# The first RMSNorm of a decoder trunk, from scheduler-ordered code to a written order

## The chip, the cores and the metric

One NeuronCore of a Trainium2 chip runs the kernel. The metric is the device time of one execution in microseconds (us), as the median of several runs. TensorE (PE in the profile, PEld for its weight loads) multiplies, VectorE (DVE) and ScalarE (ACT) do the elementwise work, GpSimd (POOL) takes some of it, and DMAs are issued from the queues of SyncE (SP) and ScalarE. Every time below counts from the first instruction of the profiled execution.

## The reference

Two layers of a decoder trunk over 512 tokens of 1024 channels, and a last norm. Each layer is

```python
for l in range(DEPTH):
    h = rmsnorm(x, norm_mix[l])
    proj = h @ w_in[l]
    pa, pb, pc, pd = split_cols(proj, [NSA_COLS, DIL_COLS, RWKV_COLS, CONV_COLS])
    ...
    x = x + jnp.concatenate([y_a, y_b, y_c, y_d], axis=-1) @ w_out[l]
    h = rmsnorm(x, norm_ffn[l])
    x = x + conv_ffn(h, ffn_up[l], ffn_dw[l], ffn_dw_b[l], ffn_down[l])
return rmsnorm(x, norm_final)

def rmsnorm(x, g):
    xf = x.astype(jnp.float32)
    y = xf * lax.rsqrt(jnp.mean(xf * xf, axis=-1, keepdims=True) + RMS_EPS)
    return (y * g).astype(x.dtype)
```

The four mixers (sparse attention, dilated attention, RWKV-7, a convolution) read `proj`. The change concerns the first `rmsnorm` of layer 0 and what feeds it.

## The kernel before

Channels lie on partitions: x is eight tiles of 128 channels by 512 tokens, in float32. Products run on float16 pairs: a value is a high part plus a low part, and one product of 128 channels is three matmuls (`mm3`, L221 to L223: weight high x hx high, weight high x hx low, weight low x hx high). A weight tile of 128 x 1024 float32 comes by DMA into a ring of two staging buffers (`st`); `_split` makes the high part on ScalarE (L200) and the low part on VectorE (L201), into a ring of five (`hl`).

The norm works in two halves of 256 tokens. For each half, ScalarE squares the eight x tiles (L363), VectorE or GpSimd adds the squares into two accumulators (L370), TensorE sums over channels by products with ones (L383), VectorE makes the inverse root in ten small steps on 128 x 2 values (L256 to L267), and two transposes on TensorE (L387) spread it over all channels. Then per tile k: VectorE scales x into `nt` (L401, a ring of three), ScalarE casts it to the high part of hx (L402), VectorE subtracts for the low part (L403).

The projection begins with `gemm_head`: four output tiles (wa, k0, r0, v0), each in a PSUM bank of its own (two of tag g, two of tag r), over the first half of the tokens, then over the second. The next tile, over all 512 tokens, takes the first bank again, once ScalarE (L411) and VectorE (L412) have read it.

A scheduler with a timeline of its own orders all instructions: it moves them past each other by their priority and by the times that it reckons with, so the order on an engine is not that of the code. The opening is written as

```python
self.norm_begin(ip, 4, 2)
for cols in self.HALVES:
    for k in range(NK):
        a1 = k % 3 == 1
        self.norm_add(k, cols, nc.gpsimd if a1 else nc.vector, int(a1))
    self.norm_apply(self.d["gm"], hx, cols)
```

with the loads of x and the first weight splits at high priority ahead of it, all from the queue of SyncE. The tables lora, cw2 and pos go out first on the queue of ScalarE.

## Time and profile before

| what | value |
|---|---|
| times of three runs | 1353.32, 1356.33, 1356.33 us (median 1356.33) |
| profiled execution: span on the page | 1353.0 us; its own time is not listed apart, the lowest run is 0.3 above |
| TensorE busy | 1301.1 us, 96% of the span |
| VectorE / ScalarE / GpSimd busy | 67% / 45% / 9% |
| first matmul of the projection | 19.01 us |
| first matmul behind the head | 42.30 us |

Busy time of TensorE is its modelled occupation, not useful work at peak. An engine's idle time costs something only where the chain that ends last passes through it. The mean granted clock of TensorE over the span is 0.988 of full speed.

### The profile page before, as it was taken

What the parts mean: (1) busy time and instruction counts of PE and PEld (TensorE: products, weight loads), DVE (VectorE), ACT (ScalarE), POOL (GpSimd) and SP (SyncE); (2) the same over time, 40 slices, a digit from 0 to 9 for tenths busy, and PEclk for the clock granted to TensorE, in tenths of its full rate; (3) what the DMA queues carried; (4) which work ended last, traced back from release to release, by engine and by line L of the source; (5) the groups of instructions that cost most, each with busy time, mean ns of one, the idle gap of its engine ahead of it and who ended that gap; (6) DMA issues with size and microseconds to landing.
All of it is one profiled execution on the core that took longest, in us unless ns stands there. A gap on an engine that the chain in (4) does not pass through costs nothing.

```text
span 1353.0 us, 22896 instructions
## 1 busy us (share of the span) xinstructions
PE 1301.1 (96%) x9198; PEld 737.9 (55%) x9198; DVE 910.4 (67%) x1770; ACT 609.3 (45%) x1115; POOL 119.5 (9%) x180
## 2 busy tenths in 40 slices
PE   5999999999999999999999998999999999999996
PEld 4545567656644444444674455775584444444445
DVE  6779985777777777632277899757678677774323
ACT  5544567644544444422245345766345444443220
POOL 2000022213000000001100001223110000000110
PEclk9999989999999999999999999999999999999998
DMA  6521400022233233333333223001214333333321
GB/s 221 162 79 59 125 26 10 1 71 94 93 94 109 93 109 94 102 120 118 109 129 124 66 79 102 10 3 32 78 49 128 105 103 100 106 93 102 98 86 63
DMA packets 41866, 119.97 MB, mean 89 GB/s; under 512 B 4896, under 2 KB 11680, under 8 KB 41760
## 3 DMA queue, kind: packets, MB, share of 16 engines
q1 hardware_dynamic: 35136, 110.50, 26.2%
q10 hardware_dynamic: 6624, 8.01, 1.8%
q8 instruction: 72, 1.18, 0.4%
q14 instruction: 34, 0.28, 0.1%
HBM read 114.30 MB, written 4.19 MB: 88 GB/s over the span
## 4 chain that ended last, share of the span: by engine, by line
PE 77%; DVE 15%; ACT 3%; DMA 2%; issue 2%; SPq 0%; ACTq 0%; DVEq 0%
PE g L222 20%; PE g L223 20%; PE g L221 20%; DVE cacc L733 4%; DVE hl L201 3%; PE v L900 3%; PE t L889 2%; PE s L869 2%; PE r L556 1%; DMA st<-in_wi_dram 1%; ACT hl L200 1%; PE r L222 1%; PE r L223 1%; DVE e L872 1%; PE r L221 1%
## 5 line engine op out<-in xcount | busy, mean ns | idle before, releaser
L221 PE MATMUL g<-hx,hl 128*128 128x512 f16 (+1 forms) x1024 | 373.7, 368 | 4.2 <-ACT hx L402 3.7
L222 PE MATMUL g<-hx,hl 128*128 128x512 f16 (+1 forms) x1024 | 374.5, 368 | 1.0 <-DVE hx L403 0.9
L201 DVE SCALAR_TENSOR_TENSOR hl<-st,hl 128x1024 f16<-128x1024 f32 (+2 forms) x200 | 239.9, 1199 | 201.0 <-ACT hl L200 200.7
L223 PE MATMUL g<-hx,hl 128*128 128x512 f16 (+1 forms) x1024 | 374.9, 368 | 0.0
L200 ACT ACTIVATE hl<-st 128x1024 f16<-128x1024 f32 (+2 forms) x200 | 206.0, 1031 | 272.7 <-PE g L223 227.7
L221 PEld LDWEIGHTS <-hl 128*128 128x128 f16 x1724 | 170.6, 99 | 162.9 <-issue 7.5
L223 PEld LDWEIGHTS <-hl 128*128 128x128 f16 x1724 | 169.8, 98 | 157.8 <-issue 2.4
L222 PEld LDWEIGHTS <-hl 128*128 128x128 f16 x1724 | 170.2, 99 | 155.2 <-issue 2.9
L222 PE MATMUL g<-act,hl 128*128 128x512 f16 (+1 forms) x396 | 140.7, 355 | 0.0
L223 PE MATMUL g<-act,hl 128*128 128x512 f16 (+1 forms) x396 | 140.7, 355 | 0.0
L221 PE MATMUL g<-act,hl 128*128 128x512 f16 (+1 forms) x396 | 140.7, 355 | 0.0
L733 DVE SCALAR_TENSOR_TENSOR cacc<-gl,d_cdw,cacc 128x511 f32<-128x511 f32 (+14 forms) x120 | 89.8, 748 | 1.4
L370 POOL TENSOR_TENSOR acc<-acc,sq 128x256 f32<-128x256 f32 (+1 forms) x38 | 44.0, 1157 | 465.9 <-ACT sq L363 409.8
L887 POOL TENSOR_SCALAR e<-e,den 128x512 f32<-128x512 f32 (+3 forms) x96 | 55.9, 596 | 316.6 <-DVE den L879 208.0
L1006 DVE SCALAR_TENSOR_TENSOR x<-g,x 128x512 f32<-128x512 f32 (+1 forms) x62 | 34.9, 568 | 67.2 <-PE g L223 67.2
L1089 ACT CAST act<-u 128x512 f16<-128x512 f32 x44 | 27.2, 618 | 114.0 <-DVE u L1087 114.0
L872 DVE CUSTOM_DVE_ANT_0 e<-s,con 128x512 f32<-128x512 f32 (+3 forms) x96 | 46.7, 487 | 33.7 <-PE s L869 25.0
L1085 ACT ACTIVATE fth<-u 128x512 f32<-128x512 f32 x44 | 27.6, 628 | 82.9 <-DVE u L1082 82.9
L1082 DVE SCALAR_TENSOR_TENSOR u<-g,d_fdw,u 128x510 f32<-128x510 f32 x84 | 62.8, 748 | 2.7
L1080 ACT ACTIVATE u<-g,par,d_fdw 128x512 f32<-128x512 f32 x84 | 64.0, 762 | 0.0
L1081 DVE SCALAR_TENSOR_TENSOR u<-g,d_fdw,u 128x511 f32<-128x511 f32 x84 | 62.5, 744 | 0.0
L876 ACT ACTIVATE e<-e,mx 128x512 f32<-128x512 f32 (+3 forms) x96 | 53.2, 556 | 16.2 <-DVE mx L874 16.1
(265 smaller groups left out, 1634.3 us busy)
## 6 DMA issues: line engine op xcount, KB each, us to landing
st<-in_up_dram SPq DMA_DIRECT2D x88, 512.0 KB, 3.5
st<-in_wi_dram SPq DMA_DIRECT2D x40, 512.0 KB, 3.4
st<-in_dn_dram SPq DMA_DIRECT2D x32, 512.0 KB, 3.5
st<-in_wo_dram SPq DMA_DIRECT2D x16, 512.0 KB, 3.5
st<-in_dn_dram SPq DMA_DIRECT2D x16, 384.0 KB, 3.1
w<-in_cw_dram ACTq DMA_DIRECT2D x16, 256.0 KB, 4.1
st<-in_wv_dram SPq DMA_DIRECT2D x8, 396.0 KB, 3.1
x<-in_x_dram SPq DMA_DIRECT2D x16, 128.0 KB, 3.5
```

The source lines that it names most:

```text
L200: nc.scalar.activation(hl[:, 0, :cols], st[:, :cols], AF.Copy, scale=SW)
L201: nc.vector.scalar_tensor_tensor(hl[:, 1, :cols], st[:, :cols], SW, hl[:, 0, :cols], op0=ALU.mult, op1=ALU.subtract)
L221: nc.tensor.matmul(ps, hl[:, 0, w], hx[:, 0, cols], start=start, stop=False)
L222: nc.tensor.matmul(ps, hl[:, 0, w], hx[:, 1, cols], start=False, stop=False)
L223: nc.tensor.matmul(ps, hl[:, 1, w], hx[:, 0, cols], start=False, stop=stop)
L733: nc.vector.scalar_tensor_tensor(acc[:, s:512], gl[:, 0:512 - s], wj, acc[:, s:512], op0=ALU.mult, op1=ALU.add)
L872: nc.vector.tensor_tensor_reduce(es[i], ps[:, o:o + w], mask[:, 384 - 128 * t:512], op0=ALU.add, op1=ALU.max, scale=1.0, scalar=-3e38, acc ...
L876: nc.scalar.activation(es[i], es[i], AF.Exp, scale=SC, bias=mx[:, i:i + 1], accum_out=den[:, i:i + 1])
L887: nc.gpsimd.tensor_scalar(es[i], es[i], den[:, i:i + 1], 1.0, op0=ALU.mult, op1=ALU.mult)
L1080: nc.scalar.activation(u, ps, AF.Identity, scale=w[:, 88 + ch:89 + ch], bias=self.p("fb", ch))
L1081: stt(u[:, 1:512], ps[:, 0:511], w[:, 44 + ch:45 + ch], u[:, 1:512], op0=ALU.mult, op1=ALU.add)
L1082: stt(u[:, 2:512], ps[:, 0:510], w[:, ch:ch + 1], u[:, 2:512], op0=ALU.mult, op1=ALU.add)
```

## The change

The opening of layer 0 moves into a function `open_x` inside a region in which the scheduler keeps the written order on each engine. In it, the first half of x is loaded from two queues in turn; the identity part of the constants, the parameters and two weight tiles follow, then the second half of x. Six of the eight squares of the first half are added by VectorE, alternating between the two accumulators, and the last two go as tiles of their own through the column sums (the ring of squares grows from four to six). The ten steps of the root stand in a row. The scaling, casts and low parts of the first half are interleaved with the two weight splits and with the squares of the second half; two of the low parts and all six adds of the second half are GpSimd's. The other constants and lora, cw2 and pos are loaded behind that. The second half then goes through the unchanged `norm_apply`. `layer_params` is cut into three functions that do the same for the later layers. Comments were dropped throughout.

```diff
+    def split_hi(self, st, cols):
+        nc = self.nc
         hl = self.whl.tile([128, 2, 1024], F16, tag="hl", name=self.n("hl"))
         nc.scalar.activation(hl[:, 0, :cols], st[:, :cols], AF.Copy, scale=SW)
-        nc.vector.scalar_tensor_tensor(hl[:, 1, :cols], st[:, :cols], SW, hl[:, 0, :cols],
-                                       op0=ALU.mult, op1=ALU.subtract)
-        return hl
+        return hl, lambda: nc.vector.scalar_tensor_tensor(hl[:, 1, :cols], st[:, :cols], SW, hl[:, 0, :cols],
+                                                          op0=ALU.mult, op1=ALU.subtract)
...
-        if l == 0:
-            self.nc.sync.dma_start(self.con[:, 128:], self.a["con"][:, 128:])
...
-            with tc.high_priority():
-                for i, cols in enumerate(self.HALVES):
-                    for k in range(NK):
-                        nc.sync.dma_start(self.x[k][:, cols], a["x"][:, k, cols])
-                    if i == 0:
-                        nc.sync.dma_start(self.con[:, :128], a["con"][:, :128])
-                        self.load_par(0)
-                    for _ in range(W_AHEAD):
-                        self.ready.append(self._split(*self.todo.pop(0)))
-            self.layer_params(0)
-            self.norm_begin(ip, 4, 2)
-            for cols in self.HALVES:
-                for k in range(NK):
-                    a1 = k % 3 == 1
-                    self.norm_add(k, cols, nc.gpsimd if a1 else nc.vector, int(a1))
-                self.norm_apply(self.d["gm"], hx, cols)
+            with tc.manual_schedule():
+                self.open_x(ip, hx)
...
+    def open_x(self, ip, hx):
+
+        nc, a = self.nc, self.a
+        h0, h1 = self.HALVES
+        load = lambda eng, k, cols: eng.dma_start(self.x[k][:, cols], a["x"][:, k, cols])
+        for k in range(NK):
+            load((nc.sync, nc.scalar)[k % 2], k, h0)
+        nc.sync.dma_start(self.con[:, :128], a["con"][:, :128])
+        self.load_par(0)
+        st = [self.w_load(*self.todo.pop(0)) for _ in range(2)]
+        for k in range(NK):
+            load(nc.sync, k, h1)
+        self.layer_consts()
+        self.norm_begin(ip, 6, 2)
+        for k in range(NK):
+            self.norm_add(k, h0, nc.vector if k < NK - 2 else None, k % 2)
+        hl0, lo0 = self.split_hi(st[0], 1024)
+        rb = self.norm_rb(h0)
+        nts = []
+        for k in range(NK + 1):
+            if k < NK:
+                nts.append(self.norm_mul(k, self.d["gm"], rb, h0))
+                nc.scalar.copy(hx[k][:, 0, h0], nts[k])
+                for i in {4: (0,), 5: (1, 2), 6: (3, 4), 7: (5, 6, 7)}.get(k, ()):
+                    self.norm_add(i, h1, nc.gpsimd, i % 2)
+            if k:
+                (nc.vector, nc.gpsimd)[k < 5 and k % 2 == 0].tensor_tensor(
+                    hx[k - 1][:, 1, h0], nts[k - 1], hx[k - 1][:, 0, h0], op=ALU.subtract)
+            if k == 1:
+                lo0()
+                self.ready.append(hl0)
+            if k == 4:
+                self.ready.append(self._split(None, 1024, st[1]))
+        for _ in range(2):
+            self.ready.append(self._split(*self.todo.pop(0)))
+        nc.sync.dma_start(self.con[:, 128:], a["con"][:, 128:])
+        self.layer_loads(0)
+        self.spread_done = None
+        self.norm_apply(self.d["gm"], hx, h1)
```

TensorE around the column sums of the second half (s is their bank, acc the accumulators, hl a split weight tile, g and r the banks of the head's tiles), before:

```order
L378 LDWEIGHTS zero
L378 MATMUL s_262<-zero 128x2
L383 MATMUL s_262<-ones,acc_165 128x1 x2
L383 MATMUL s_262<-ones,acc_166 128x1 x2
L221 LDWEIGHTS hl_119
L221 MATMUL g_344<-hx_79,hl_119 128x256
L221 LDWEIGHTS hl_132
L221 MATMUL g_345<-hx_79,hl_132 128x256
```

and now, further back, between the second and the third tile of the head:

```order
L226 LDWEIGHTS hl_262
L226 MATMUL r_352<-hx_79,hl_262 128x256
L395 MATMUL s_277<-ones,acc_155 128x1 x2
L225 LDWEIGHTS hl_267
L225 MATMUL r_353<-hx_79,hl_267 128x256
L226 LDWEIGHTS hl_267
L226 MATMUL r_353<-hx_79,hl_267 128x256
L395 MATMUL s_277<-ones,acc_156 128x1 x2
L227 LDWEIGHTS hl_262
L227 MATMUL r_352<-hx_79,hl_262 128x256
L225 LDWEIGHTS hl_262
L225 MATMUL r_352<-hx_80,hl_262 128x256
```

The sums stood ahead of all products; now they stand among the first products of the third and the fourth tile (r). From the last row of the sums to the transposes that spread the second root there are 41 products over 256 columns, which now stand between the two.

VectorE at the scaling of the second half (nt the scaled tile, hx the pair, t the spread root), before:

```order
L267 SCALAR_TENSOR_TENSOR y_271<-a_272,y_271 128x2
L403 TENSOR_TENSOR hx_86<-nt_238,hx_86 128x256
L401 SCALAR_TENSOR_TENSOR nt_285<-x_98,d_gm_141,t_263 128x256
L401 SCALAR_TENSOR_TENSOR nt_289<-x_99,d_gm_141,t_263 128x256
L401 SCALAR_TENSOR_TENSOR nt_293<-x_100,d_gm_141,t_263 128x256
L403 TENSOR_TENSOR hx_79<-nt_285,hx_79 128x256
L403 TENSOR_TENSOR hx_80<-nt_289,hx_80 128x256
L401 SCALAR_TENSOR_TENSOR nt_297<-x_101,d_gm_141,t_263 128x256
L403 TENSOR_TENSOR hx_81<-nt_293,hx_81 128x256
L401 SCALAR_TENSOR_TENSOR nt_301<-x_102,d_gm_141,t_263 128x256
L401 SCALAR_TENSOR_TENSOR nt_305<-x_103,d_gm_141,t_263 128x256
```

and now:

```order
L271 SCALAR_TENSOR_TENSOR y_286<-a_287,y_286 128x2
L206 SCALAR_TENSOR_TENSOR hl_342<-st_340,hl_342 128x1024
L410 SCALAR_TENSOR_TENSOR nt_300<-x_98,d_gm_131,t_278 128x256
L419 TENSOR_TENSOR hx_79<-nt_300,hx_79 128x256
L410 SCALAR_TENSOR_TENSOR nt_304<-x_99,d_gm_131,t_278 128x256
L419 TENSOR_TENSOR hx_80<-nt_304,hx_80 128x256
L410 SCALAR_TENSOR_TENSOR nt_308<-x_100,d_gm_131,t_278 128x256
L419 TENSOR_TENSOR hx_81<-nt_308,hx_81 128x256
L410 SCALAR_TENSOR_TENSOR nt_312<-x_101,d_gm_131,t_278 128x256
L419 TENSOR_TENSOR hx_82<-nt_312,hx_82 128x256
L410 SCALAR_TENSOR_TENSOR nt_316<-x_102,d_gm_131,t_278 128x256
```

Two or three scaled tiles stood ahead of their low parts; now each low part follows its own scaled tile, and a weight split (hl) stands between the root and the first of them.

TensorE at the end of the head, before:

```order
L221 LDWEIGHTS hl_331
L221 MATMUL r_347<-hx_86,hl_331 128x256
L222 LDWEIGHTS hl_331
L222 MATMUL r_347<-hx_86,hl_331 128x256
L223 LDWEIGHTS hl_331
L223 MATMUL r_347<-hx_86,hl_331 128x256
L221 LDWEIGHTS hl_336
L221 MATMUL g_559<-hx_79,hl_336 128x512
L222 LDWEIGHTS hl_336
L222 MATMUL g_559<-hx_79,hl_336 128x512
```

and now:

```order
L227 LDWEIGHTS hl_175
L227 MATMUL g_350<-hx_86,hl_175 128x256
L226 LDWEIGHTS hl_225
L226 MATMUL g_351<-hx_86,hl_225 128x256
L227 LDWEIGHTS hl_225
L227 MATMUL g_351<-hx_86,hl_225 128x256
L226 LDWEIGHTS hl_262
L226 MATMUL r_352<-hx_86,hl_262 128x256
L227 LDWEIGHTS hl_262
L227 MATMUL r_352<-hx_86,hl_262 128x256
L226 LDWEIGHTS hl_267
L226 MATMUL r_353<-hx_86,hl_267 128x256
```

Before, only the fourth tile is left there: the last product of the first tile (g_344) stands 33 products ahead of the end. Now all four tiles run through the same k, and the last product of the first tile (g_350, the first rows) stands six ahead of the end. The next tile, over 512 columns, follows in both.

## Rows read from the trace of the kernel before

**Rows 1.** The page's first part: busy us, share, instructions.

```profile
PE 1301.1 (96%) x9198; PEld 737.9 (55%) x9198; DVE 910.4 (67%) x1770; ACT 609.3 (45%) x1115; POOL 119.5 (9%) x180
```

**Rows 2.** Windows, start:end and length, then busy us of each engine (instructions), PEclk, DMA.

```profile
19.01:42.30 23.29, 22.96 (x196) 19.77 (x196) 17.87 (x46) 11.68 (x21) 0.76 (x4) 1.00 0.44 144
42.30:1353.00 1310.70, 1273.69 (x8986) 714.11 (x8983) 883.79 (x1703) 587.22 (x1073) 111.77 (x152) 0.99 0.27 85
```

**Rows 3.** Timeline of TensorE: column sums of two tiles, first matmuls.

```profile
8.80 1.87 PE L383 MATMUL s<-ones,acc 128*128 128x1 f32 x8 [7.01 <-DVE acc L370]
...
19.01 0.59 PE L221 MATMUL g<-hx,hl 128*128 128x256 f16 x2
```

**Rows 4.** Timeline of VectorE, first root: start us, us, instruction, idle before.

```profile
10.70 0.16 DVE L256 TENSOR_SCALAR u<-s 128x2 f32<-128x2 f32 x1 [1.96 <-PE s L383]
...
11.72 0.23 DVE L263 SCALAR_TENSOR_TENSOR y<-a,y 128x2 f32<-128x2 f32 x1
...
16.07 0.15 DVE L267 SCALAR_TENSOR_TENSOR y<-a,y 128x2 f32<-128x2 f32 x1
...
17.15 0.47 DVE L401 SCALAR_TENSOR_TENSOR nt<-x,d_gm,t 128x256 f32<-128x256 f32 x1
```

**Rows 5.** Timeline of TensorE: spacing of matmuls early and late, first of 512 columns.

```profile
22.43 0.42 PE L222 MATMUL g<-hx,hl 128*128 128x256 f16 x1
22.64 0.38 PE L223 MATMUL g<-hx,hl 128*128 128x256 f16 x1
...
42.08 0.27 PE L222 MATMUL r<-hx,hl 128*128 128x256 f16 x1
42.19 0.27 PE L223 MATMUL r<-hx,hl 128*128 128x256 f16 x1
42.30 0.38 PE L221 MATMUL g<-hx,hl 128*128 128x512 f16 x1
```

**Rows 6.** Timeline of ScalarE, squares of both halves; DMA issues of x (count, KB, us to landing).

```profile
4.02 0.42 ACT L363 ACTIVATE acc<-x 128x256 f32<-128x256 f32 x1 [0.59 <-DMA x<-in_x_dram]
...
7.87 0.75 ACT L363 ACTIVATE sq<-x 128x256 f32<-128x256 f32 x2 [0.77 <-DMA x<-in_x_dram]
...
13.53 1.63 ACT L363 ACTIVATE sq<-x 128x256 f32<-128x256 f32 x5
...
x<-in_x_dram SPq DMA_DIRECT2D x16, 128.0 KB, 3.5
```

**Rows 7.** Timeline of VectorE and ScalarE: scaling, casts and low parts, second half.

```profile
30.16 1.26 DVE L401 SCALAR_TENSOR_TENSOR nt<-x,d_gm,t 128x256 f32<-128x256 f32 x3 [0.73 <-PE t L387]
30.68 1.19 ACT L402 CAST hx<-nt 128x256 f16<-128x256 f32 x3 [2.61 <-DVE nt L401]
31.35 0.75 DVE L403 TENSOR_TENSOR hx<-nt,hx 128x256 f16<-128x256 f32 x2
...
35.32 0.98 DVE L403 TENSOR_TENSOR hx<-nt,hx 128x256 f16<-128x256 f32 x2
```

**Rows 8.** Timeline: weight split and evacuation of the first tile, end of the head.

```profile
38.90 1.06 ACT L200 ACTIVATE hl<-st 128x1024 f16<-128x1024 f32 x1 [3.06 <-DMA w<-in_cw_dram]
...
39.99 1.23 DVE L201 SCALAR_TENSOR_TENSOR hl<-st,hl 128x1024 f16<-128x1024 f32 x1 [3.69 <-ACT hl L200]
41.13 0.74 DVE L412 SCALAR_TENSOR_TENSOR wa<-g,d_mu,wa 128x511 f32<-128x511 f32 x1
```

**Rows 9.** Timeline: adds of the second half on GpSimd and VectorE.

```profile
14.62 0.72 POOL L370 TENSOR_TENSOR acc<-acc,sq 128x256 f32<-128x256 f32 x1 [1.54 <-ACT sq L363]
14.78 0.85 DVE L370 TENSOR_TENSOR acc<-acc,sq 128x256 f32<-128x256 f32 x1
```

**Rows 10.** Windows around a fall of the granted clock (columns as in rows 2).

```profile
329.00:333.50 4.50, 2.37 (x23) 2.13 (x21) 4.50 (x10) 2.58 (x6) 1.60 (x2) 1.00 0.39 118
333.50:337.00 3.50, 3.50 (x19) 2.43 (x17) 3.50 (x14) 1.61 (x4) 0.00 (x0) 0.52 0.47 150
```

**Rows 11.** Timeline of TensorE: first product that reads lora.

```profile
47.57 1.12 PE L440 MATMUL r<-wa,lora 64*128 64x512 f32 x2
```

More of the change, by code (lines that the diff above doesn't have):

```diff
@@ L194, in w_split, with _split @@
             return self._split(src, cols)
-    def _split(self, src, cols):
+    def _split(self, src, cols, st=None):
         nc = self.nc
-        st = self.w_load(src, cols)
+        hl, lo = self.split_hi(self.w_load(src, cols) if st is None else st, cols)
+        lo()
+        return hl
+    def split_hi(self, st, cols):
+        nc = self.nc
         hl = self.whl.tile([128, 2, 1024], F16, tag="hl", name=self.n("hl"))
         nc.scalar.activation(hl[:, 0, :cols], st[:, :cols], AF.Copy, scale=SW)
-        nc.vector.scalar_tensor_tensor(hl[:, 1, :cols], st[:, :cols], SW, hl[:, 0, :cols],
-                                       op0=ALU.mult, op1=ALU.subtract)
-        return hl
+        return hl, lambda: nc.vector.scalar_tensor_tensor(hl[:, 1, :cols], st[:, :cols], SW, hl[:, 0, :cols],
+                                                          op0=ALU.mult, op1=ALU.subtract)
     def plan(self, items, depth):
@@ L314, in layer_params, with ptile, layer_loads @@
     def layer_params(self, l):
-        nc, a = self.nc, self.a
-        t = lambda name, shape: self.cp.tile(shape, F32, tag=name, bufs=1, name=self.n(name))
-        if l:
-            self.load_par(l)
+        self.load_par(l)
+        self.layer_loads(l)
+        self.layer_consts()
+    def ptile(self, name, shape):
+        return self.cp.tile(shape, F32, tag=name, bufs=1, name=self.n(name))
+    def layer_loads(self, l):
+        nc, a, t = self.nc, self.a, self.ptile
         self.lora = t("lora", [128, 512])
@@ L324, in layer_params, with layer_consts @@
         nc.scalar.dma_start(self.pos, a["pos"][l])
-        v = nc.gpsimd
+    def layer_consts(self):
+        t = self.ptile
+        v = self.nc.gpsimd
         self.d = {}
@@ L394, in order, with norm_mul @@
             mybir.DependencyClass.NoSync, mybir.DependencyReason.DATA), reason="order")
+    def norm_mul(self, k, g, rb, cols):
+        t = self.np.tile([128, 256], F32, tag="nt", bufs=3, name=self.n("nt"))
+        self.nc.vector.scalar_tensor_tensor(t, self.x[k][:, cols], g[:, k:k + 1], rb, op0=ALU.mult, op1=ALU.mult)
+        return t
     def norm_apply(self, g, hx, cols):
@@ L399, in norm_apply @@
         for k in range(NK):
-            t = self.np.tile([128, 256], F32, tag="nt", bufs=3, name=self.n("nt"))
-            nc.vector.scalar_tensor_tensor(t, self.x[k][:, cols], g[:, k:k + 1], rb, op0=ALU.mult, op1=ALU.mult)
+            t = self.norm_mul(k, g, rb, cols)
             nc.scalar.copy(hx[k][:, 0, cols], t)
```

1 line of the change is left out of this document (added).

## The prediction

> **What bounds the kernel now.** The page's first part comes first: TensorE is busy 96% of the span and VectorE two thirds [rows 1]. Cut in stretches, TensorE has 22.96 us of work in the 23.29 us between its first matmul and the end of the head (the first four output tiles, by halves of the tokens), and 1273.69 of the 1310.70 us behind it [rows 2]. So what matters of an opening is when TensorE starts and whether it stays fed. It starts at 19.01 [rows 3]; nearly everything before that is the first half's norm. The timeline shows where that time goes: the root's ten small VectorE steps begin at 10.70, five of them take 1.02 us, and the tenth starts at 16.07, since other VectorE work stands between them [rows 4]. The head ends at 42.30, where the first matmul over 512 columns (the tile behind the head) starts without a gap [rows 5]. I measure the change at that point.
>
> **First half, earlier.** The first x tile is squared at 4.02 in both kernels: its DMA is still the first. Before, the last two squares run at 7.87 to 8.62 [rows 6]. Now no constant stands ahead of the eight x issues and two queues share them; the last leaves about 2.6, lands 3.5 later [rows 6] at 6.1, and the square ends about 7.0. The table load moves behind four issues on ScalarE and ends near 3.8, hidden by the first landing. Two of the adds become products: four tiles go through the column sums instead of two, at 1.87/2 = 0.93 us a tile [rows 3], 3.7 us from about 6.5: the root begins at 10.3, not 10.70, so little is won here. Unbroken, its ten steps take 10 x 0.205 = 2.05 and end at 12.4, not 16.22; from there to the first scaled tile (nt) it was 17.15 - 16.22 = 0.93 [rows 4]. So nt starts at 13.4, 3.75 earlier, and the first matmul about 14.4, 4.6 earlier.
>
> **First half, its length.** VectorE now has eight nt (0.39 apart), six low parts of hx (0.33) and two weight splits (41.13 - 39.99 = 1.14) in a row [rows 7, 8]: 3.1 + 2.0 + 2.3 = 7.4. In this order four of them wait for ScalarE: the second split stands behind a cast, a square and its own high part (1.06), some 1.8; three low parts right behind their cast, some 0.9 together. The first half is written at 13.4 + 7.4 + 2.7 = 23.5. TensorE has two tiles' work, 48 matmuls, for these ten microseconds.
>
> **Second half, later.** Its squares, done by 16.1 before (five from 13.53, the last right after) [rows 6], now stand between and behind the casts on ScalarE: the third about 22.1, the last about 24.4. All six adds are GpSimd's, at 0.72 each [rows 9]: 4.3 us in series, to 26.5. TensorE, in order, has the column sums of the second half ahead of nearly all of tiles three and four: it can run four of their matmuls, and does one accumulator's sums after the fifth add and the other's after the sixth, each 0.93, to 27.9. Then come 41 matmuls, and only then the transposes that spread the second root. At 0.11 apart (the upper clock level, as at 42.08 to 42.19) that is 4.5 us; at 0.21 apart (the lower, as at 22.43 to 22.64) it is 8.7 [rows 5]. The rest is ready by then: two splits from 25.4 to 27.8, root to 29.9, and the fifth split, whose load waits for a staging buffer until 26.6, at about 32.5. With 0.5 for the transposes nt of the second half starts at 33.0 (upper level) or 37.2 (lower throughout); before it started at 30.16 [rows 7]. This is the disputed term. In this profile the clock is granted at 0.52 from 333.5 for 3.5 us, after a stretch in which TensorE was busy 2.37 of 4.50 us [rows 10]. Here TensorE does about 2.3 us of work (four matmuls and two sums) in the 4.4 between 23.5 and 27.9, the same share. I therefore take the lower level for the first 3.4 us: 16 matmuls, then 25 in 2.7, 6.1 in all, nt at 34.6. [...]
>
> **Second half, its pace.** Before, VectorE ran two or three nt ahead and the casts hid behind them: from 30.16 to 36.3, 6.1 us for eight tiles [rows 7]. In the written order each low part follows its nt at once, so VectorE waits for each cast: nt to cast 30.68 - 30.16 = 0.52, cast 0.41, low part 0.33 and a handover of 0.05, 1.31 a tile [rows 7], 10.5 for eight. TensorE's four tiles take 12 x 0.11 = 1.31 per k, so it neither catches up nor waits much; behind the last low part it has eight matmuls, 0.9. The head ends at 34.6 + 11.4 = 46.0, before at 42.30.
>
> **A bank that comes free late.** TensorE takes all four tiles through one k after the other, so the first tile ends six matmuls before the head does, not 33 as before. The tile behind the head needs that tile's bank. Its evacuation stands behind a weight split whose ring slot the same tile frees: high part 1.06, low part 1.14, then the shifted add 0.74 [rows 8], with handovers 3.1, less six matmuls (0.65): a gap of about 2.5. Before, this chain (38.90 to 41.87) lay beside the other tiles' matmuls and cost nothing. So the tile behind the head starts at 48.5 against 42.30: **+6.2 us**.
>
> **Costed at nothing.** Lora and the small tables, loaded about 26 instead of 0.7, are first read at 47.57 [rows 11]; the big constants land near 26 and are first read later still. If that cover were gone, the price would be a landing, 3.5. The parameters land earlier than before, so their twelve GpSimd steps are done when the first low part comes. GpSimd's two low parts of hx are not in the trace: from 0.42, as on VectorE, to 0.72, as its adds; I take 0.72, and neither end is on the path. A VectorE add beside a GpSimd add took 0.85 [rows 9], twice an undisturbed low part; up to 1.5 us so lost beside six adds falls into VectorE's slack before 33.0. The instructions behind the head are those of before with a few exchanged; for that I keep 1 us either way. All of the delay should reach the end: TensorE is 97% busy behind the head, and whatever it waits for there starts from its own tiles.
>
> **Sum.** At the lowest +4.6 (nt at 33.0), at the highest +8.8 (nt at 37.2), taken +6.2. The profiled execution's span is 1353.0, 0.3 under the fastest run and 3.3 under the median of 1356.33, which two of three runs show; I put the sum on the median: 1362.5. By the span it would be 1359.2.
>
> **Rivals.**
> *Upper clock level throughout* (1360.9): the same chain with 4.5 us for the 41 matmuls. For it: TensorE's first half is dense enough to have raised the clock once; against: the idle stretch behind it.
> *No change* (about 1356): the late head is made up: of TensorE's 37 us of waits behind it [rows 2] some may be for work that doesn't hang on the head, and the gap of 2.5 may close. Against: no such work is in sight; the transfers are early enough.
> *Faster* (1351.7): the 4.6 us of the earlier start survive. It decides at GpSimd's last add. Counted back from 42.30 by 2.5 for the gap, 11.4 for the second half, 0.5 and 4.5 for the 41 matmuls and 0.93 for a sum, the two kernels are even if that add ends at 22.5, and the 4.6 are kept whole if it ends at 17.9; I have 26.5. For it: the squares' inputs lie ready from 15. Against: the order on ScalarE and on TensorE, which no timing changes.
> *Worse* (1366): the lower level through all 41 matmuls, or VectorE's losses to GpSimd on the path.
>
> **Chances and range.** Forecast 0.45, upper level 0.22, no change 0.20, faster 0.06, worse 0.07. What a measurement of this kernel can tell from no change is about 0.3%, 4.1 us, as its runs differ by 3.0. The forecast and the worse case are slower; of the upper-level case (+4.6) two thirds are, the rest reads as the same; of the no-change case a few are on either side. Slower 0.67, same 0.26, faster 0.07. The range runs from inside the no-change case, 1354, to the highest sum with the 1 us behind the head and the noise of the runs, 1369.
>
> **What would show it.** First nt at 13 to 14, first matmul 14 to 15 (the early gain); GpSimd's six adds ending at 26 to 27, and TensorE's second column sums right behind; first nt of the second half at 33 to 37; VectorE alternating nt and low part 1.3 apart; TensorE idle 2 to 3 us ahead of the first matmul over 512 columns, which comes at 46.5 to 51. If that matmul comes before 42.3, the forecast is wrong at the second half; if it comes at 48 and the time doesn't move, it is wrong at the carrying to the end.

## The result, and the profile after

The changed kernel takes 1362.74 us, the median of four runs (1361.84 to 1365.25); the kernel before 1356.13 (four runs, 1353.32 to 1356.33). The ratio is 1.0057, with a 95% interval of 1.0045 to 1.0069: slower by 6.6 us, where 6.2 was forecast. The profiled execution after is the longest of its four, 1365.25 with a span of 1363.5, so its 10.5 us over the span of before overstates the difference. Places in the opening are compared below, not spans.

The page's first part and the timeline's rows of VectorE and TensorE that answer to [rows 1], [rows 3] and [rows 4] (start, duration, engine, line; in brackets the idle time before and what ended it):

```profile
PE 1308.8 (96%) x9206; PEld 739.7 (54%) x9206; DVE 910.5 (67%) x1764; ACT 608.7 (45%) x1115; POOL 125.8 (9%) x184
```

```profile
9.74 0.16 DVE L260 TENSOR_SCALAR u<-s 128x2 f32<-128x2 f32 x1 [3.29 <-PE s L395]
...
11.60 0.16 DVE L271 SCALAR_TENSOR_TENSOR y<-a,y 128x2 f32<-128x2 f32 x1
12.62 0.87 DVE L410 SCALAR_TENSOR_TENSOR nt<-x,d_gm,t 128x256 f32<-128x256 f32 x2 [0.86 <-PE t L399]
...
22.47 0.70 DVE L1242 TENSOR_TENSOR hx<-nt,hx 128x256 f16<-128x256 f32 x1 [0.16 <-ACT hx L1238]
24.35 2.89 DVE L206 SCALAR_TENSOR_TENSOR hl<-st,hl 128x1024 f16<-128x1024 f32 x2 [1.17 <-ACT hl L205]
...
34.91 0.48 DVE L410 SCALAR_TENSOR_TENSOR nt<-x,d_gm,t 128x256 f32<-128x256 f32 x1 [3.21 <-PE t L399]
35.86 0.43 DVE L419 TENSOR_TENSOR hx<-nt,hx 128x256 f16<-128x256 f32 x1 [0.47 <-ACT hx L418]
36.20 0.48 DVE L410 SCALAR_TENSOR_TENSOR nt<-x,d_gm,t 128x256 f32<-128x256 f32 x1
...
47.01 1.23 DVE L206 SCALAR_TENSOR_TENSOR hl<-st,hl 128x1024 f16<-128x1024 f32 x1 [1.71 <-ACT hl L205]
48.15 0.74 DVE L428 SCALAR_TENSOR_TENSOR wa<-g,d_mu,wa 128x511 f32<-128x511 f32 x1
```

```profile
13.59 0.37 PE L225 MATMUL g<-hx,hl 128*128 128x256 f16 x1 [1.08 <-ACT hx L1238]
...
26.22 0.61 PE L395 MATMUL s<-ones,acc 128*128 128x1 f32 x4 [1.03 <-POOL acc L382]
...
27.88 0.61 PE L395 MATMUL s<-ones,acc 128*128 128x1 f32 x4 [0.82 <-POOL acc L382]
28.35 0.27 PE L227 MATMUL r<-hx,hl 128*128 128x256 f16 x1
...
34.49 0.38 PE L399 MATMUL t<-con,y 128*128 128x128 f32 x2
...
46.27 0.27 PE L227 MATMUL r<-hx,hl 128*128 128x256 f16 x1
48.96 0.39 PE L225 MATMUL g<-hx,hl 128*128 128x512 f16 x1 [2.42 <-DVE wa L428]
```

What the reader is to see: the root's ten steps now stand in a row (9.74 to 11.76) and the first matmul comes 5.4 us earlier than in [rows 3]. Then TensorE waits for GpSimd's accumulator (1.03 and 0.82 us), does 41 matmuls between 28.35 and 34.49, and only then the transposes; VectorE's brackets say the same from the other side: 3.21 us idle ahead of the second half's first product, ended by the transposes. That product starts at 34.91, 4.75 later than in [rows 7]. At the end of the head TensorE waits 2.42 us for the first tile's bank, and the next tile starts at 48.96 against 42.30 in [rows 5]: +6.7.

GpSimd's timeline, and the windows of the two stretches in which the clock fell (start:end, length, busy time and count by engine, then the granted clock):

```profile
14.01 1.65 POOL L1242 TENSOR_TENSOR hx<-nt,hx 128x256 f16<-128x256 f32 x1 [3.38 <-ACT hx L1238]
16.43 0.67 POOL L1242 TENSOR_TENSOR hx<-nt,hx 128x256 f16<-128x256 f32 x1 [0.77 <-ACT hx L1238]
21.30 6.52 POOL L382 TENSOR_TENSOR acc<-acc,sq 128x256 f32<-128x256 f32 x6 [4.21 <-ACT sq L375]
```

```profile
29.50:32.90 3.40, 3.40 (x18) 2.42 (x17) 2.03 (x6) 0.94 (x1) 0.00 (x0) 0.50 0.33 125
32.90:34.90 2.00, 2.00 (x20) 1.82 (x19) 0.00 (x0) 0.00 (x0) 0.00 (x0) 1.00 0.65 234
46.50:48.90 2.40, 0.04 (x1) 0.00 (x0) 1.89 (x3) 2.40 (x4) 0.00 (x0) 1.00 0.62 162
49.00:50.00 1.00, 1.00 (x5) 0.46 (x6) 1.00 (x2) 1.00 (x3) 0.00 (x0) 0.98 0.99 270
50.00:53.30 3.30, 3.30 (x9) 1.21 (x8) 2.01 (x4) 0.74 (x2) 0.00 (x0) 0.50 0.92 271
```

The granted clock is 0.50, the lower level, from 29.5 to 32.9, after TensorE had waited twice for GpSimd, and again from 50.0 to 53.3, just behind the wait for the bank. The second stretch was not in the forecast. In a second profile of the same kernel (e11_again) the first one is absent.

### The profile page after: what moved, and what is told of

Its sections match the earlier page's. It is cut to its first block, busy times and chain, and to the rows that moved or that the text cites. A ratio compares the mean times of both kernels' runs of the same rounds, so it can differ in the third digit from the quotient of the medians.

```text
span 1363.5 us, 22903 instructions
## 1 busy us (share of the span) xinstructions
PE 1308.8 (96%) x9206; PEld 739.7 (54%) x9206; DVE 910.5 (67%) x1764; ACT 608.7 (45%) x1115; POOL 125.8 (9%) x184
## 4 chain that ended last, share of the span: by engine, by line
PE 74%; DVE 16%; ACT 4%; issue 3%; DMA 2%; ACTq 0%; POOL 0%; DVEq 0%; POOLq 0%
PE g L226 19%; PE g L225 19%; PE g L227 19%; DVE cacc L749 4%; DVE hl L206 3%; PE v L916 3%; PE t L905 2%; ACT hl L205 2%; PE s L885 2%; DMA st<-in_wi_dram 2%; PE r L572 1%; DVE e L888 1%; PE r L227 1%; PE r L226 1%; PE r L225 1%
## 5 line engine op out<-in xcount | busy, mean ns | idle before, releaser
L382 POOL TENSOR_TENSOR acc<-acc,sq 128x256 f32<-128x256 f32 (+1 forms) x40 | 47.6, 1194 | 461.9 <-ACT sq L375 405.8
```

## The experiments

Theory: the second half's inverse root is late (GpSimd's additions, then 41 matmuls ahead of the transposes), the first tile's bank comes free late, and all of that reaches the end. Main rival: the time is lost behind the head or in the clock, and what happens in the opening is cover.

The table gives starts on each kernel's profiled timeline: first matmul, first product of the second half, last matmul of the head, first matmul of the next tile; then one ScalarE instruction well behind the head (the evacuation of tile gd) as a landmark, and the median and its ratio to the kernel before run beside it.

| kernel | matmul | product | head's last | next tile | landmark | median us | ratio, 95% interval |
|---|---|---|---|---|---|---|---|
| before | 19.01 | 30.16 | 42.19 | 42.30 | 78.64 | 1354.4 to 1356.1 | 1 |
| changed | 13.59 | 34.91 | 46.27 | 48.96 | 87.64 | 1362.74 | 1.0057 (1.0045 to 1.0069) |
| e11_again | 13.63 | 33.27 | 44.63 | 47.31 | 85.98 | 1362.53 | 1.0061 (1.0045 to 1.0077) |
| e1_pace | 13.64 | 34.95 | 46.53 | 47.15 | 83.64 | 1360.63 | 1.0035 (1.0021 to 1.0049) |
| e2_squares | 13.80 | 31.94 | 44.28 | 48.10 | 85.07 | 1362.96 | 1.0052 (1.0036 to 1.0069) |
| e3_evac | 13.67 | 33.32 | 44.68 | 45.86 | 89.25 | 1365.99 | 1.0077 (1.0065 to 1.0090) |
| e4_order | 13.97 | 31.90 | 44.33 | 47.02 | 85.06 | 1362.05 | 1.0044 (1.0029 to 1.0060) |
| e5_consts | 16.62 | 36.59 | 47.94 | 50.63 | 88.67 | 1365.95 | 1.0073 (1.0055 to 1.0091) |
| e7_warm | 14.57 | 34.54 | 45.90 | 48.59 | 88.32 | 1364.65 | 1.0073 (1.0059 to 1.0088) |
| e9_all | 13.77 | 29.34 | 44.53 | 44.63 | 80.43 | 1360.25 | 1.0038 (1.0027 to 1.0050) |
| e10_direct | 13.68 | 32.47 | 45.45 | 48.13 | 84.94 | 1361.74 | 1.0049 (1.0031 to 1.0067) |
| e12_queues | 22.50 | 32.79 | 45.58 | 45.69 | 82.11 | 1359.26 | 1.0031 (1.0020 to 1.0043) |
| e13_fill | 15.65 | 30.24 | 46.65 | 46.76 | 82.45 | 1358.38 | 1.0024 (1.0014 to 1.0034) |
| e14_warm0 | 19.99 | 31.42 | 43.00 | 43.18 | 80.51 | 1357.38 | 1.0014 (1.0006 to 1.0023) |

The landmark's lag behind 78.64 and the lag of the medians can be laid side by side: changed 9.0 and 6.6 (again: 7.3 and 8.1), e1 5.0 and 5.1, e2 6.4 and 7.4, e3 10.6 and 10.5, e4 6.4 and 6.5, e5 10.0 and 10.3, e7 9.7 and 9.0, e9 1.8 and 4.6, e10 6.3 and 6.1, e12 3.5 and 4.8, e13 3.8 and 4.0, e14 1.9 and 2.0. What is lost by 80 us is found at the end, in all but e9 within 2.4 us and mostly within 1.

One thing has to be kept apart in the table. Around 30 us, where the 41 matmuls stand, the granted clock is at the lower level for 3.4 us in the first profile of the changed kernel (the one in the result above) and in those of e1 and e10, and at the upper level in those of e11 (the changed kernel's second profile), e2, e3, e4, e5 and e7. That alone moves the places behind it by 1.65 us (see e11), so a place should be compared with the profile of the changed kernel that had the same level there.

### The second half later or earlier

**e4_order**, one order on TensorE.

```
 for k in range(NK):
-    self.mm3(ps[:, cols], hl, k, hx[k], cols, k == 0, k == NK - 1)
+    mm = self.mm3(ps[:, cols], hl, k, hx[k], cols, k == 0, k == NK - 1)
...
+    if self.hold is not None and i == n - 1 and k == 0:
+        self.order(mm, self.hold)      # fourth tile behind the transposes
```

> One order on TensorE is added: the first half's fourth output tile (24 matmuls) goes behind the transposes of the second norm's inverse root, so some 23 matmuls stand between the column sums and the transposes in place of 41. My theory (the second half starts where the 41 matmuls let the transposes through, not where the sums or the root end): sums end 28.4 as before, root about 31, first product at 31.3 to 32.5 in place of 34.9; VectorE's last low part comes by as much earlier, but TensorE then has 24 + 96 matmuls at 0.11 left, so the head's end moves by 1 to 2.5 us: 1361 (1360.0 to 1362.0). Rival, that GpSimd's last addition and the root decide and the matmuls are cover: no change of the first product beyond 0.5 us, 1362.7.

Measured: sums at 28.26, transposes at 31.12, first product at 31.90 in place of 34.91 and the head's last matmul 1.9 earlier. Set against e11, whose clock was at the upper level here as e4's was, the product is 1.4 earlier and the head's last matmul only 0.3. So the 41 matmuls, not the sums or the root, held the start of the second half, but its start hardly moves the end of the head. The windows from about 28.4 us to the head's end, of the kernel before, of e11 and of e4, show why:

```profile
28.40:42.30 13.90, 13.90 (x130) 12.47 (x128) 9.34 (x22) 6.60 (x13) 0.76 (x4) 1.00 0.40 124
28.20:44.70 16.50, 15.82 (x145) 13.98 (x145) 9.40 (x27) 4.71 (x10) 0.65 (x4) 1.00 0.22 76
28.70:44.40 15.70, 15.70 (x146) 14.04 (x145) 9.30 (x27) 4.71 (x10) 0.65 (x4) 1.00 0.27 87
```

TensorE works without a wait in e4, and with 0.68 us of waiting in e11: it has the same matmuls to do in either order, some 15 more than the kernel before has left at about that time, although it started 5 us earlier. In the time little is left of the edit: 1.0044, against 1.0057 and 1.0061 with overlapping intervals.

**e2_squares**, squares and additions of the second half placed earlier.

```
-for i in {4: (0,), 5: (1, 2), 6: (3, 4), 7: (5, 6, 7)}.get(k, ()):
+for i in {1: (0, 1, 2), 3: (3, 4, 5), 4: (6, 7)}.get(k, ()):
```

> The squares of the second half and their additions on GpSimd are placed earlier (behind products 1, 3 and 4 of the first half in place of 4 to 7); nothing else is edited. My theory (the column sums of the second half wait for GpSimd's last addition at 27.8 us, and the transposes stand behind them and 41 matmuls): the sums are done by about 24 us, TensorE's waits of 1.03 and 0.82 us for GpSimd go, VectorE's root follows the two weight splits at about 27 us, the first product of the second half starts at about 30 to 31 us in place of 34.9, and the next tile's first matmul falls from 48.96 to about 45: 1358.7 us (1357.5 to 1360.5). Rival, that what is given back lies behind the head (later weights and constants): no change, 1362.7.

The first product came at 31.94, 3.0 us earlier than in the first profile of the changed kernel and 1.3 earlier than in e11, but the head's last matmul only 0.35 earlier than in e11, and the time stayed. The timeline of VectorE, and the window of TensorE from the second half's sums to the head's end:

```profile
30.80 1.23 DVE L206 SCALAR_TENSOR_TENSOR hl<-st,hl 128x1024 f16<-128x1024 f32 x1 [1.71 <-ACT hl L205]
31.94 0.48 DVE L410 SCALAR_TENSOR_TENSOR nt<-x,d_gm,t 128x256 f32<-128x256 f32 x1
...
45.02 2.36 DVE L206 SCALAR_TENSOR_TENSOR hl<-st,hl 128x1024 f16<-128x1024 f32 x2 [2.70 <-ACT hl L205]
47.30 0.74 DVE L428 SCALAR_TENSOR_TENSOR wa<-g,d_mu,wa 128x511 f32<-128x511 f32 x1
```

```profile
22.30:44.40 22.10, 22.10 (x183) 18.89 (x183) 13.57 (x34) 7.47 (x14) 0.65 (x4) 1.00 0.50 170
```

The fifth weight's split, whose load had only just landed, now stands directly ahead of the first product. But that did not hold the head's end: TensorE never waits from 22.3 on. Its matmuls stand 0.21 apart up to 26.8, the lower level, and 0.11 behind that, so what the early sums gave back went into slower matmuls. (The clock column reads 1.00 there all the same: the trace has no record of the clock before 26.9, and the spacing tells the level.) And the planner (the scheduler that orders all work behind the hand-placed opening) put two splits, not one, ahead of the first tile's evacuation, so the wait for the bank grew from 2.42 to 3.55 us. The expectation of -4 fails at these two, not at the sums.

**e10_direct**, no additions on GpSimd.

```
-self.norm_add(i, h1, nc.gpsimd, i % 2)
+self.norm_add(i, h1, None, i % 2)
```

> The second half's eight squares go straight into TensorE's column sums; its six additions on GpSimd are gone (12 more 1-column matmuls at 0.15 to 0.3 us, 2 to 3 us of TensorE); nothing else is edited. My theory: the last sums come with the last square at 23.4 us plus the splits ahead on TensorE, by 26.5 in place of 28.4, GpSimd's 6.5 us no longer run beside VectorE's splits (2.89 back to 2.37 us), and 32 matmuls are left between sums and transposes in place of 41: first product at about 32.5 in place of 34.9, head's end -1.5, the bank gap as it is: 1361.2 (1360 to 1362.5). Rival, that GpSimd's slow additions are off the path: no change, 1362.7; or that the 12 extra matmuls cost as much as they save, 1363.

Measured: first product 32.47 as expected; the head's last matmul 0.8 earlier than in the first profile of the changed kernel, which like this one has 3.4 us at the lower level here, since the 12 further sums took TensorE 3.0 us. VectorE's two splits take 2.36 us again:

```profile
24.44 2.36 DVE L206 SCALAR_TENSOR_TENSOR hl<-st,hl 128x1024 f16<-128x1024 f32 x2 [1.46 <-ACT hl L205]
```

In the changed kernel the pair took 2.89, and the six additions 6.52 us, not six times 0.72 as in [rows 9]. Taken one by one there, the second split and the last two additions are the slow ones; the first four took 0.72 to 0.91:

```profile
24.42 1.75 POOL L382 TENSOR_TENSOR acc<-acc,sq 128x256 f32<-128x256 f32 x1
25.50 1.75 DVE L206 SCALAR_TENSOR_TENSOR hl<-st,hl 128x1024 f16<-128x1024 f32 x1
26.12 1.70 POOL L382 TENSOR_TENSOR acc<-acc,sq 128x256 f32<-128x256 f32 x1
```

The Trainium skill, "SBUF — State Buffer", section "Who interferes with whom", says that a VectorE instruction with two inputs in SBUF and a GpSimd instruction that reads SBUF get in each other's way; the rows agree, on both engines. They take turns there: the fifth addition ends 0.59 us behind the end of the first split (25.58), the second split 1.08 behind that addition, the last addition 0.57 behind that split, each about its own time.

### The end of the head

**e1_pace**, products two ahead of their low parts.

```
-self.norm_apply(self.d["gm"], hx, h1)
+rb = self.norm_rb(h1)
+nts = []
+for k in range(NK + 2):
+    if k < NK:
+        nts.append(self.norm_mul(k, self.d["gm"], rb, h1))
+        nc.scalar.copy(hx[k][:, 0, h1], nts[k])
+    if k > 1:
+        nc.vector.tensor_tensor(hx[k - 2][:, 1, h1], nts[k - 2], hx[k - 2][:, 0, h1], op=ALU.subtract)
```

> The second half's products on VectorE run two ahead of their low parts (no other edit), so VectorE no longer waits 0.47 us for each cast and its pace falls from 1.29 to about 0.9 us a tile. My theory: TensorE, not VectorE, is then the pace (12 matmuls at 0.11 = 1.31 us a tile of x, all four output tiles still taken tile of x by tile of x), so the end of the head moves by no more than the last cast and low part, 0 to -1 us: 1362.2 (1361.5 to 1362.9). Rival, that VectorE's alternation sets the head's end and its 0.4 us a tile come off: -3 us, 1359.7.

VectorE's last product came at 39.99 in place of 43.93, and the head's last matmul at 46.53, no earlier than 46.27: TensorE's 12 matmuls are the pace, as the theory says. But it missed something. TensorE no longer waits at each tile of x, so the four output tiles finish one after another, and the first is taken out while the others still run:

```profile
45.08 0.67 ACT L427 ACTIVATE wa<-g,d_om 128x512 f32<-128x512 f32 x1
```

```profile
47.15 0.39 PE L225 MATMUL g<-hx,hl 128*128 128x512 f16 x1 [0.34 <-DVE wa L428]
```

The wait for the bank fell from 2.42 to 0.34 us and the clock stayed at the upper level behind it. The landmark comes 4.0 earlier than in the first profile of the changed kernel, which has the lower level in the 41 matmuls as this one has, and 2.3 earlier than in the second. The lag of the median falls from 6.6 and 8.1 to 5.1; the intervals of the ratios just overlap.

**e3_evac**, the first tile taken out ahead of the next weight's split.

```
+if i == 6:
+    self.evac = (e0, e1)               # ScalarE's and VectorE's evacuation of tile wa
...
+if ev[0] is not None:
+    self.order(i, ev[0])               # the split's high part behind it; the low part likewise
```

> Only the order behind the head is changed: the first output tile is taken out of its PSUM bank (ScalarE 0.67, VectorE 0.74 us) ahead of the split of the weight that takes over its buffer (1.06 and 1.23 us), not behind it. My theory: TensorE's wait of 2.42 us for the bank shrinks by the split's share to about 0.9 us and the rest follows one for one: -1.5 us, 1361.2 (1360.6 to 1362.0). Rival, that this wait is covered by a later one for weights: no change, 1362.7; then the later wait is seen within the next two tiles.

The wait fell to 0.91 as expected, and the next tile started at 45.86, the second earliest of all versions built on the changed kernel. Yet this is the slowest kernel of the study. Its windows show where:

```profile
60.00:64.00 4.00, 3.11 (x15) 1.21 (x13) 3.83 (x6) 2.15 (x5) 0.00 (x0) 1.00 0.70 218
64.00:66.00 2.00, 1.72 (x11) 1.49 (x12) 1.26 (x2) 2.00 (x5) 0.00 (x0) 0.85 0.83 235
66.00:69.00 3.00, 2.79 (x20) 0.74 (x18) 2.00 (x12) 1.36 (x3) 0.00 (x0) 0.50 0.96 338
69.00:72.00 3.00, 2.07 (x23) 0.96 (x19) 1.23 (x3) 0.79 (x3) 0.00 (x0) 0.50 0.56 198
72.00:76.10 4.10, 4.10 (x13) 1.78 (x14) 3.24 (x7) 1.41 (x4) 0.00 (x0) 0.56 0.13 54
```

TensorE waits from 63 us on for later work (0.9 us for squares, 1.3 us in four waits more), and the clock is at the lower level from 65.4 to 75.6. The edit also lets fewer weights be split ahead within the head (`self.depth` set to 1, not shown above), which moved the load and split of the following weights, and the planner wrote the next stages in another order. The rival's later wait is there; between the next tile (3.6 late) and the landmark (10.6) it loses 7 us, and how much of them is the new order's and how much the clock's was not separated.

### The clock

**e11_again**, the changed kernel once more, no edit.

> The changed kernel once more, for a second profile of it. My theory: what the engines' order sets is the same to 0.2 us (first matmul 13.6, column sums of the second half 28.4, its first product 34 to 35, the next tile's first matmul 48 to 49), and the stretch at the lower clock right behind TensorE's 2.4 us wait for the bank is there again; the median stays at 1362.7 (1361.5 to 1364). Rival, that the stretch behind the wait is chance: it is absent, and the second profile is 1.5 to 3.5 us shorter with it.

The windows of the same two places, and TensorE's first matmul of the next tile:

```profile
28.00:32.00 4.00, 4.00 (x38) 3.63 (x39) 2.77 (x11) 1.06 (x1) 0.00 (x0) 1.00 0.43 158
44.70:47.30 2.60, 0.20 (x2) 0.00 (x0) 1.93 (x3) 2.60 (x4) 0.00 (x0) 1.00 0.63 189
47.30:50.30 3.00, 2.98 (x8) 1.04 (x9) 3.00 (x4) 1.80 (x4) 0.00 (x0) 0.50 0.94 259
```

```profile
47.31 0.61 PE L225 MATMUL g<-hx,hl 128*128 128x512 f16 x1 [2.41 <-DVE wa L428]
```

The 41 matmuls ran at the upper level this time and everything behind them came 1.65 earlier. So that stretch at the lower level is chance from run to run, after the same waits. The Trainium skill, "TensorE: Matmul & The Clock Gate", section "What's actually happening", says that the gate's watch isn't restarted by a kernel; two profiles of one program that differ in this way agree with it, though they don't show that this is the reason. The stretch behind the wait for the bank was there in both. Over all profiles with a wait of 2.4 us or more at that place it follows in five of seven (not in e7 and e10), and right behind the next tile's start it is absent in the four versions of the changed kernel that wait 0.91 us or less (e1, e3, e9, e13).

**e7_warm**, TensorE kept at work from the start by matmuls of a zero tile.

```
+vb = self.vbank()
+for i in range(90):
+    nc.tensor.matmul(vb[:, 0:128], self.zero, self.zero, start=i == 0, stop=i == 89)
 self.norm_begin(ip, 6, 2)
```

> 90 matmuls of a zero tile (128 columns each, their result is never read) keep TensorE at work from the start to about 10 us; the rest is the changed kernel. My theory: the granted clock is then at the upper level at the first real matmul (13.6 us) in place of 22.6, so the first two output tiles keep pace with their inputs, but these end with the last low part at 23.2 us anyway and the third and fourth wait for their weights' splits at 25.5 and 27.5 us: the first product of the second half at 34 to 35 us, no more than 0.9 us earlier, 1362.3 (1361.3 to 1363.0). Rival, that the lower level up to 22.6 us is the real cost: the 42 matmuls in it at 0.21 in place of 0.11 give back 4.4 us, 1358.3.

```profile
7.00:10.00 3.00, 3.00 (x50) 3.00 (x47) 0.00 (x0) 0.00 (x0) 1.94 (x9) 1.00 0.93 335
10.00:13.90 3.90, 1.46 (x13) 1.30 (x13) 1.93 (x11) 1.06 (x1) 1.02 (x4) 0.96 0.81 256
13.90:24.10 10.20, 7.40 (x32) 3.98 (x32) 8.15 (x16) 6.19 (x17) 4.13 (x5) 0.51 0.44 140
```

The clock did rise: 53 of the zero matmuls take the 5.4 us up to 7.0, the next 37 the 2.2 us behind it. It fell again at 13.9, after TensorE had been busy 1.46 of 3.90 us. The expectation was wrong on the clock, and its time (1361.3 to 1363.0) was missed; on what the clock is worth it can't be judged by this run, in which the first product came 0.4 earlier than in the first profile of the changed kernel and 1.3 later than in e11, the one with the same level in the 41 matmuls. Between the next tile (6.3 late) and the landmark (9.7) this kernel lost 3.4 us more.

### Parts of the change by themselves

**e5_consts**, the layer's constants first on ScalarE's queue.

```
+self.layer_loads(0)
...
 for k in range(NK):
     load((nc.sync, nc.scalar)[k % 2], k, h0)
...
-self.layer_loads(0)                   # from behind the other constants
```

> The three constants of the layer (lora, cw2, pos: 328 KB) are issued first again on ScalarE's queue, ahead of x, as in the kernel before; the large block of constants and all else stay as in the changed kernel. My theory (constants are cover on either side): the last x of the first half lands 0.3 to 1.0 us later than 6.4 us, the first product moves with it, and the second half, which starts behind the 41 matmuls, by the same or less: 1363.2 (1362.0 to 1364.0). Rival, that moving them is what cost the 6.6 us (a late lora or a collision with the weights at 20 to 27 us): 1359 or less.

Worse by 3, not 0.5. ScalarE's timeline (ACTq is its queue):

```profile
0.73 0.42 ACTq L329 DMA_DIRECT2D lora<-in_lora_dram  x1
...
2.14 3.47 ACTq L1221 DMA_DIRECT2D x<-in_x_dram  x4
5.64 1.28 ACT L375 ACT_TABLE_LOAD   x1 [5.64 <-DMA pos<-in_pos_dram]
6.93 0.72 ACT L375 ACTIVATE acc<-x 128x256 f32<-128x256 f32 x2
```

In the changed kernel the four issues of x take 1.86 us from 0.73 and the first square starts at 3.92. Behind three other issues they take 3.47, and ScalarE's table load and squares stand behind them on the same engine. All of the 3.0 us is there at the first matmul, and 3.3 at the next tile, set against e11, whose 41 matmuls ran at the upper level as they did here. Moving the constants later is what makes the second queue pay.

**e12_queues**, the kernel before with x's first half from two queues.

```
-nc.sync.dma_start(self.x[k][:, cols], a["x"][:, k, cols])
+(nc.sync, nc.scalar)[k % 2 if i == 0 else 0].dma_start(self.x[k][:, cols], a["x"][:, k, cols])
```

> On the kernel before, one part alone: x's first half loaded from two queues, all else left to the planner. My theory (the early start is not what limits the head: VectorE must do 16 products, 16 low parts, four splits and two roots by 36 us either way): x lands 1 to 2 us earlier, but VectorE takes the first root behind the second half's additions and a split, so the first matmul comes at 18 to 20 us and the next tile at 42 to 43.5: 1356.5 (1355 to 1358). Rival, that the two queues are a gain that the hand order gave away: 1354 or less.

The first matmul came at 22.50, 3.5 later than before: lora's issue stands ahead of x on ScalarE's queue, the squares start at 7.29 in place of 4.02, and the planner put two splits and the second half's additions ahead of the root's end. So by itself this part is a loss (1.0031); together with the root in one piece and the constants later it makes the 5.4 us of earlier start; no run takes the root's part alone.

### Versions that try to win

**e9_all** joins early squares, root and sums ahead of the last two splits, the pace of e1, and the fifth and sixth weights' splits behind the last low part and the first evacuation; it sets `self.depth` to 0 within the head, not shown here.

```
+rb = self.norm_rb(h1)
+for s in st:
+    self.ready.append(self._split(None, 1024, s))
...
+self.gates = [(g0, g1)]               # cast and low part ahead of the fifth weight's split
```

> All the placements that the single edits point to at once: squares of the second half early, its column sums and inverse root ahead of the last two weight splits on VectorE, its products two ahead of the low parts, the fifth weight's split behind the last low part, and the first tile's evacuation ahead of the sixth weight's split. My theory: root at 23.3 to 25.3, splits to 27.8, first product at 28 us; TensorE gets the third tile at 26.5 and the fourth at 27.8, ends the first half at about 31 and the second 10.5 us later, at 41.5, the gap under 1 us: next tile at 42.4 in place of 48.96, as before the change (42.30): 1356 (1354.5 to 1358.5). Rival, that about half of the 6.6 us is set behind the head and stays: 1359.5 or more.

From 22 us on TensorE never waits, and the bank costs nothing:

```profile
22.00:44.60 22.60, 22.60 (x185) 19.34 (x185) 17.69 (x39) 11.34 (x19) 0.94 (x5) 1.00 0.65 220
```

But its matmuls stand 0.21 apart until 27.4 (0.11 from 27.5; the column's 1.00 covers a stretch without a record of the clock, as in e2), so the next tile comes at 44.63, not 42.4. The landmark is 1.8 late, the time 4.6: nearly 3 us are lost far behind the head. Which step does it is open. In the profile the clock was granted at 0.51 from 157.0 to 160.5 and at 0.50 from 266.3 to 269.7, with TensorE busy throughout, where the kernel before stood at 1.00 (155 to 158 and 263 to 267); but that kernel had 6.8 us at 0.50 from 176.5, and this one 3.4 there, so the clock explains only some of it, and one profile doesn't tell for the other executions.

**e13_fill**: e9 with 110 zero matmuls from the start and 14 behind each tile of x in the first output tile.

```
...
+vb = self.vbank()
+for i in range(self.fill):
+    d = self.nc.tensor.matmul(vb[:, 0:128], self.zero, self.zero, start=i == 0, stop=i == self.fill - 1)
+    if i == 0:
+        self.order(d, mm)
```

> The version with all placements, and TensorE kept at work by matmuls of a zero tile that nobody reads: 110 from the start, and 14 behind each tile of x in the first output tile of the first half, where it waits for inputs. My theory: in that version TensorE never waits from 22 us on, and what is left of the loss is the lower clock up to 27.5 us; with the clock at its upper level from the first matmul the first two tiles end with the last low part, the third and fourth start with their splits at 26 to 27.5, and the next tile comes at about 41 us in place of 44.6 (before: 42.3): 1357.7 (1356 to 1359.5). Rival, that the clock falls all the same or that the extra matmuls delay the real ones: 1360 or more.

```profile
15.60:20.20 4.60, 4.55 (x38) 4.16 (x38) 3.37 (x6) 3.90 (x13) 2.80 (x5) 0.54 0.33 115
20.20:46.70 26.50, 25.98 (x279) 23.61 (x277) 20.18 (x42) 13.91 (x23) 4.61 (x9) 1.00 0.56 192
```

The clock is up from 20.2 on, 7 us earlier than in e9, but 84 of the zero matmuls then stand ahead of real ones, and the first matmul came 1.9 later. The next tile came at 46.76, not at about 41: the rival's delay. The time lies in the expected range all the same, which is luck, as the step that was to give it failed. At 1358.38 it is the fastest version built on the changed kernel, and still slower than before.

**e14_warm0**: the kernel before with 64, 90 and 30 zero matmuls where TensorE is idle (ahead of and behind the first sums, behind the first transposes).

```
+if self.fill:
+    self.warm(self.fill.pop(0), mm)    # behind the sums; likewise behind the transposes
```

> The kernel before, with matmuls of a zero tile that nobody reads where TensorE is idle at the start: 64 ahead of the first column sums, 90 behind them, 30 behind the transposes of the first root. My theory: TensorE's 23.29 us from first matmul (19.01) to the next tile (42.30) hold some 19 matmuls at the lower clock, up to 23.0 us; with the clock at its upper level from the first one 2.0 us come off, since the engine never waits there: next tile at 40.3, 1353.4 us where the kernel before has 1355.4 (ratio 0.9985, 0.997 to 1.0). Rival, that the clock falls behind the extra matmuls as it did where TensorE was starved in the changed kernel, or that the inputs then set the pace: no change, ratio 1.000 (0.999 to 1.001).

```profile
18.80:22.20 3.40, 3.40 (x25) 2.79 (x23) 3.40 (x11) 1.97 (x4) 0.00 (x0) 0.50 0.65 242
```

The theory falls: the clock drops to the lower level at 18.8, just as the real work begins, the inputs come no earlier, and the time is 1.0014. The first product of the second half, at 31.42, had waited 2.45 us for transposes that stood behind matmuls of the first half, against 0.73 in [rows 7]. No version here beats the kernel before.

## Why the prediction was right, step by step

**First half.** Products from 12.62 (forecast 13.4), first matmul 13.59 (14.4), last low part done at 23.17 (23.5). Right; the root in one piece took 2.02 us, 2.05 were worked out, and x landed a little earlier.

**GpSimd's additions.** Forecast end 26.5, measured 27.82. The term was mis-sized: 4.3 us were taken for the six, 6.5 it was, most of the excess in the two additions beside VectorE's weight splits (1.75 and 1.70). The prediction had counted such a loss for VectorE alone. But the additions began 0.9 earlier than forecast, and the sums behind the last one took 0.6 us, not 1.4. So the sums were done at about 28.4, forecast 27.9: three errors cancel there but for 0.5, which is luck.

**The 41 matmuls.** 6.1 us taken, 6.14 measured, with the lower level for 3.4 us of it; the second profile had 4.5 and no such stretch. So the forecast and its rival with the upper level throughout are the same program on two runs: next tile +6.7 in one (+6.2 forecast) and +5.0 in the other (+4.6 forecast). The path was named wrong in part. The prediction lets the transposes behind the 41 matmuls set the end of the head; e4 shows that their place sets when the second half starts (1.4 us) but not when the head ends (0.3). From the sums on TensorE's own work is the path, and the sum came out because both paths are nearly equally long: TensorE waits only 0.68 us on this stretch in e11.

**The pace.** 1.31 a tile forecast, 1.29 measured. The prediction named VectorE's waits for casts as the cause and TensorE as nearly even. e1 takes VectorE's waits away and the head's end stays: TensorE binds. The pace mattered in another way, through the order in which the four tiles finish.

**The bank.** 2.5 forecast, 2.42 measured; e1 and e3 take most of it away by its two causes.

**Carried to the end.** Right in kind. One for one holds from the landmark on in most versions, and on e1 the time follows. Mis-sized is what lies between: 1 us either way was kept for the stretch behind the head; in both profiles the landmark is 2.3 us later than the next tile's lag says, of which the 3.3 us at half clock behind the wait for the bank account for 1.65. The forecast of 6.2 is near the measured 6.6 in part by luck: the term behind the head was missing 2.3 us, and the sum made it up by 1.6 us for the lower clock in the 41 matmuls, which only one of the two profiles has.

**The rivals.** No change and faster are excluded by the intervals. The upper level throughout is what the second profile shows in the 41 matmuls, and its median is no lower. That the order of the work behind the head costs time was kept as 1 us; e3, e7 and e9 lose 3 to 7 us there (e9 only behind the landmark), to waits, clock and order together, in other kernels. How much of the changed kernel's own 6.6 us is lost there is not settled; it need not be more than the 2.3 named above.

## What to carry to other kernels

An earlier start of the engine that binds is worth nothing if it has done no more by the time its later inputs come: count how much work it has left at a fixed time (here some 15 matmuls more at 28.4 us, after a start 5.4 us earlier), not when its first matmul runs. Where work is placed by hand, look at what stands in each queue ahead of the short instruction that others wait for (here an evacuation behind a weight split), and then whether the engine that binds waits for it at all: the two transposes behind 41 matmuls delayed a start but hardly an end. A change of a few microseconds in front of a planned schedule orders all that follows anew, so judge it at a landmark behind the stage and by several versions, not by one time, and compare places only between profiles whose clock stood alike.

## What the runs showed of the hardware that was not expected

- DMA issues on ScalarE's queue hold up its compute: four issues of x took 1.86 us as the first on the queue and 3.47 behind three others (e5), and the table load and the squares waited for them (first square at 3.92 and 6.93).
- Matmuls of zeros raise the granted clock (up at 7.0 in e7), but it did not last: it fell at 13.9, after 3.90 us with 1.46 of work, and stayed down for 10.2 us in which TensorE was busy 7.40. In e14 it fell at 18.8, after 1.97 us of work in the 2.30 from 16.5.
- A wait of 2.4 us for one bank was followed by 3.3 us at half clock in both profiles of the changed kernel, so such a wait can cost 4 us, not 2.4 (an estimate: half of the 3.3 us on top of the wait). In e7 and e10 the same wait was not followed by it.
- GpSimd's additions of 128x256 took 0.72 to 0.91 us, and 1.75 and 1.70 beside VectorE's weight splits of 128x1024, one of which took 1.75 in place of 1.23; a subtraction of the same size took 1.65 where it began 0.1 us behind a VectorE weight split of 1.22.
